# First queries projected ahead of the later values, second modulation vector staged in the context's place

## Chip, cores and metric

The kernel runs on one core of one Trainium2 chip. The metric is the device time of one execution in microseconds (us). The core has a matrix engine (PE, with weight loads shown apart as PEld), a vector engine (DVE), a scalar engine (ACT), GpSimd (POOL), and SyncE (SP), whose queue issues the loads here. Each engine takes its own instructions in the order in which the built program holds them, and an instruction that waits holds up what stands behind it on the same engine.

## The reference

Two trunk layers over 512 latent tokens of width 1024, with a prefix of 256 context tokens. What touches the change is the entry of layer 0:

```python
sh1, sc1, g1, sh2, sc2, g2 = adaln_params(c, mod_w[i], mod_b[i])      # silu(c) @ w + bias, 6 vectors of 1024
h  = modulate(rms_norm(x, norm_g[i, 0]), sh1, sc1)                    # latent tokens
hc = modulate(rms_norm(ctx, norm_g[i, 0]), csh1, csc1)                # context tokens
proj = h @ w_in                                                       # queries of 8 heads, keys and values of 4
q_a = apply_rope(rms_norm(q_a, q_g), cos, sin)                        # heads 0-3, global; keys of this group likewise
k_a = apply_rope(rms_norm(k_a, k_g), cos, sin)
q_b, k_b = apply_rope(q_b), apply_rope(k_b)                           # heads 4-7, windowed, no norm
o_a = attend(q_a, [k_ctx, k_a], [v_ctx, v_a]);  o_b = window_attention(q_b, ...)
y = concat([o_a, o_b]) @ w_out
x = x + g1 * rms_norm(y, norm_g[i, 1])                                # then a gated ConvFFN with sh2, sc2, g2
```

Layer 1 replaces attention by a Fourier mixing. All matrix products are done in three passes on a high and a low part (`mm3`: high by high, high by low, low by high), so every weight and activation is first split: ACT casts the high part (`wh`), DVE or POOL subtracts for the low part (`wl`).

## The kernel before

The input projection of layer 0 runs in two parts. The first (the loop over `START`) makes the modulated latent tokens `hh`/`hl` and context tokens `ch`/`cl` and, as they come, the keys and values of the global group. Then the loop over `kind` (line 835 and on) does three column groups of 256: `kb` (keys of the windowed heads), `vb` (their values) and `qa` (queries of heads 0 and 1). A group takes blocks of two token tiles: two latent blocks, and for `kb` and `vb` a third one of context. A block is 48 matmuls of 128x256 into one PSUM tile `mm`. The `qa` blocks also carry side work: `keys(0)` at the first of them, which transposes the first key head out of `K` (six PE transposes into two `misc` tiles), and splits it into `kh`/`kl`; `values(0)` at the second.

The keys of the global group are normalised late: `kst` holds sums of squares, `rsqrt(krs, ...)` makes the reciprocal roots in a chain of small DVE instructions, and POOL then scales the twelve 128x128 pieces of `K` by `krs` (line 796). `keys(0)` can transpose a piece only when POOL has scaled it.

Beside that runs `gate = gemv_early(...)`: two adaLN vectors (0, 2) and (0, 3) are made on DVE, eight multiply-adds of 128x1024 each (line 472; `scol` holds the activated c), with one load of 512 KB per multiply-add (line 458). The loads lie in five places in turn: three in `yT` (`yf[:, 0..2]`) and two in the place `cT` that the context tokens have left. The first vector gathers in `yf[:, 3]`, the second in `sqx`. `gemv_end` then sums over partitions on PE (line 433), and transposes back (line 443). The loop over `kind` advances this generator by `pump(gate, n)`.

`yT` is also where the queries go: `Q` is a view of it, and `q_out(0, t0, ps)` writes the rotated first queries there (`roped`, lines 741 to 765; the last step on POOL for the first block, on DVE for the second). `queries_t(0)` transposes them for head 0 (line 943), with the queries of heads 2 and 3 (`gm`) projected between.

Order: `SY` issues loads in program order, each waiting until its place is free. A scheduler places the instructions on each engine by priority of code order and by when their buffers come free; the built order is what counts.

Of the kernel before, what the change touches and what calls it, by code (L numbers as in the profile page):

```python
# [21 lines left out]
KC = D // P  # L22
# [54 lines left out]
def kernel(ctx: ExitStack, tc: tile.TileContext, a):  # L77
# [5 lines left out]
    def mk(pool, shape, dt=F32, tag=None, bufs=1):  # L83
        cnt[0] += 1
        n = nbufs.setdefault((id(pool), tag), (pool, bufs))[1]
        return pool.tile(shape, dt, tag=tag, name=f"{tag}_{cnt[0]}", bufs=n)
# [343 lines left out]
    def gemv_end(l, v, acc, pps):  # L430
        ps = mk(pps, [P, T], F32, "misc", 2)
        for j in range(4):
            PE.matmul(ps[32 * j:32 * j + 32, :256], lhsT=ones32, rhs=acc[:, j * 256:(j + 1) * 256], start=True,
                      stop=True)
        rs = acc
        S.copy(out=rs[:, :256], in_=ps[:, :256])
        yield
        gemv_out(l, v, rs, pps)
# [12 lines left out]
    def gemv_early(jobs, places, accs, pps):  # L451
        ws = {}

        def load(n):
            if n < KC * len(jobs):
                (l, v), k = jobs[n // KC], n % KC
                ws[n] = places[n % len(places)]()
                SY.dma_start(out=ws[n], in_=a["mod_r"][6 * l + v - 2, k // 2][:, k % 2, :])

        for n in range(3):  # L460
            load(n)
        yield
        for n in range(3, len(places)):
            load(n)
        yield
        ends = []
        for n in range(KC * len(jobs)):
            acc, k = accs[n // KC], n % KC
            if k == 0:
                V.tensor_scalar(out=acc, in0=ws[n], scalar1=scol[:, 0, k:k + 1], scalar2=None, op0=ALU.mult)  # L470
            else:
                V.scalar_tensor_tensor(out=acc, in0=ws[n], scalar=scol[:, 0, k:k + 1], in1=acc, op0=ALU.mult,
                                       op1=ALU.add)
            load(n + len(places))
            yield
            if k == KC - 1:
                ends.append(gemv_end(*jobs[n // KC], acc, pps))
            elif k in (1, 3):
                for e in ends:
                    next(e, None)  # L480
        yield
        for _ in range(2):
            next(ends[-1], None)
            yield
# [22 lines left out]
    def pump(it, n=1):  # L507
        for _ in range(n):
            next(it, None)
# [12 lines left out]
    with ExitStack() as es:  # L522
# [16 lines left out]
        def keys(kv, parts):  # L539
            b0 = 0  # L540
            for pt, n in parts:
                for b in range(n):
                    PE.transpose(out=pt[:, b * P:(b + 1) * P], in_=K[:, b0 + b, kv * P:(kv + 1) * P], identity=ident)
                split(kh[:, b0 * P:(b0 + n) * P], kl[:, b0 * P:(b0 + n) * P], pt[:, :n * P])
                b0 += n

        def values(kv):
            vh, vl = wpair([P, 6, P])
            split(vh, vl, Vv[:, :, kv * P:(kv + 1) * P])
            return vh, vl  # L550

        with ExitStack() as e1:
# [150 lines left out]
            for s in START.split():  # L703
                n = [int(c) for c in s[1:]]
# [24 lines left out]
            def context_place(i):  # L729
                if not ce:  # L730
                    ce.append(mk(pj, [P, KC, TC], F32, "cT").rearrange("p a b -> p (a b)").rearrange(
                        "p (n d) -> p n d", d=D))
                return ce[0][:, i, :]

            gate = gemv_early([(0, 2), (0, 3)], [lambda i=i: yf[:, i, :] for i in range(3)] + [
                lambda i=i: context_place(i) for i in range(2)],
                [yf[:, 3, :], sqx[:, 0:4, :].rearrange("p a b -> p (a b)")], pps)
# [33 lines left out]
            def k_out(dst, src, t0, is_ctx):  # L771
                if is_ctx:
                    S.copy(out=dst, in_=src)
                else:
                    roped(dst, src, t0, None)
# [23 lines left out]
            def group_weights(g):  # L799
                r = raw([P, KC, 256], a["w_in"][g])  # L800
                out = []
                for i in range(2):
                    wh, wl = wpair([P, 4, 256])
                    split(wh, wl, r[:, 4 * i:4 * i + 4, :])
                    out.append((wh, wl))
                return out

            def project(ps, ws, sh, sl, t0):
                for i in range(2):
                    tk = slice((t0 + i) * P, (t0 + i + 1) * P)  # L810
                    for k in range(KC):
                        wh, wl = ws[k // 4]
                        mm3(ps[:, i, :], sh[:, k, tk], sl[:, k, tk], wh[:, k % 4, :], wl[:, k % 4, :], k == 0,
                            k == KC - 1)
                        if k % 2:
                            yield


            def q_out(qi, t0, ps):
                dst = Q[:, t0:t0 + 2, qi * 256:(qi + 1) * 256]  # L820
                if qi < 2:

                    roped(dst, ps, t0, 0, qst[:, qi, t0:t0 + 2, :].rearrange("p a b -> p (a b)"),
                          V if qi == 0 and t0 else G)
                else:
                    roped(dst, ps, t0, None)
                if qi < 2 and t0:
                    q, r = (v[:, qi, :, :].rearrange("p t h -> p (t h)") for v in (qst, qrs))
                    V.tensor_scalar(out=q, in0=q, scalar1=1.0 / P, scalar2=EPS, op0=ALU.mult, op1=ALU.add)
                    rsqrt(r, q, qtm)  # L830
                    V.tensor_scalar(out=qsc[:, 2 * qi:2 * qi + 2, :].rearrange("p h t -> p t h"),
                                    in0=qrs[:, qi, :, :], scalar1=SCALE, scalar2=None, op0=ALU.mult)

            blocks = [(hh, hl, 0, 2), (hh, hl, 2, 4), (ch, cl, 0, 0)]
            for g, kind in enumerate(["kb", "vb", "qa"]):
                ws = group_weights(g)
                if g == 2:
                    v_kv = []
                if g == 2:
                    w_q = group_weights(3)  # L840
                for sh, sl, t0, kb in (blocks if kind[0] != "q" else blocks[:2]):
                    ps = mk(pps, [P, 2, 256], F32, "mm", 6)
                    pr = project(ps, ws, sh, sl, t0)
                    for _ in range(2):
                        pump(pr, 4)
                        pump(gate, 2 if kind == "vb" else 1)
                    if kind == "vb":
                        S.copy(out=Vv[:, kb:kb + 2, 256:512], in_=ps)
                    elif kind == "kb":
                        k_out(K[:, kb:kb + 2, 256:512], ps, t0, sh is ch)  # L850
                    else:
                        if t0 == 0:
                            keys(0, [(mk(pps, [P, T], F32, "misc", 2), n) for n in (2, 4)])
                        else:
                            v_kv.append(values(0))
                        q_out(0, t0, ps)
# [12 lines left out]
        with ExitStack() as e2:  # L869
# [80 lines left out]
            for head in range(8):  # L950
# [6 lines left out]
                for j in range(TT):  # L957
# [4 lines left out]
                    if is_a:  # L962
# [4 lines left out]
                        reg, n = ps[:, 128:896], NK  # L967
                    else:
# [12 lines left out]
                        reg, n = ps[:, 256:512 + nl], TC + nl  # L981
# [674 lines left out]
```

## Time and profile before

| What | Value |
|---|---|
| median of 3 runs | 1150.75 us (1148.4 to 1152.72) |
| the profiled execution | 1151.45 us, of which span 1149.7 us |
| mean granted TensorE clock | 0.992 |
| DVE, ACT, POOL busy | 877.7, 578.3, 174.0 us (76%, 50%, 15% of the span) |
| loads and stores | 149.51 MB, 130 GB/s over the span |

The span runs from the first to the last instruction of the profiled execution; 1.75 us of that execution's time lie around it. A busy share is an average over stages; what an edit is worth is read in its own stage, here 85 to 150 us of the span.

### The profile page before, as it was taken

What the parts mean: (1) busy time and instruction counts of PE and PEld (TensorE: products, weight loads), DVE (VectorE), ACT (ScalarE), POOL (GpSimd) and SP (SyncE); (2) the same over time, 40 slices, a digit from 0 to 9 for tenths busy, and PEclk for the clock granted to TensorE, in tenths of its full rate; (3) what the DMA queues carried; (4) which work ended last, traced back from release to release, by engine and by line L of the source; (5) the groups of instructions that cost most, each with busy time, mean ns of one, the idle gap of its engine ahead of it and who ended that gap; (6) DMA issues with size and microseconds to landing.
All of it is one profiled execution on the core that took longest, in us unless ns stands there. A gap on an engine that the chain in (4) does not pass through costs nothing.

```text
span 1149.7 us, 19092 instructions
## 1 busy us (share of the span) xinstructions
PE 1117.8 (97%) x7642; PEld 963.9 (84%) x7642; DVE 877.7 (76%) x1422; ACT 578.3 (50%) x1030; POOL 174.0 (15%) x178
## 2 busy tenths in 40 slices
PE   8999999999999999999999998989999999999995
PEld 4689988868888978887998898869887888899895
DVE  4678777765679976987998568988997498679745
ACT  4342356666665633552465445557743355256442
POOL 1236332521420000000000153500000000000023
PEclk9999999999999999999999999999999999999998
DMA  9576101075142355545525300630228123223212
GB/s 366 239 242 214 44 1 38 7 265 205 38 184 111 125 196 198 214 131 201 193 98 191 113 9 15 206 106 35 74 84 281 46 103 111 93 91 111 92 56 74
DMA packets 30881, 149.51 MB, mean 130 GB/s; under 512 B 3140, under 2 KB 7876, under 8 KB 18632
## 3 DMA queue, kind: packets, MB, share of 16 engines
q1 hardware_dynamic: 30792, 148.29, 36.5%
q8 instruction: 60, 0.98, 0.3%
q14 instruction: 29, 0.24, 0.1%
HBM read 144.08 MB, written 4.19 MB: 129 GB/s over the span
## 4 chain that ended last, share of the span: by engine, by line
PE 84%; DVE 8%; ACT 5%; issue 2%; POOL 1%; DMA 0%; DVEq 0%; SPq 0%; ACTq 0%; POOLq 0%
PE mm L99 24%; PE mm L100 23%; PE mm L101 23%; PE PT L914 1%; ACT wh L122 1%; PE mm L174 1%; PE O L99 1%; DVE md_t L291 1%; PE gm L492 1%; PE gm L99 1%; PE O L100 1%; PE gm L101 1%; PE gm L100 1%; PE O L101 1%; PE misc L180 1%
## 5 line engine op out<-in xcount | busy, mean ns | idle before, releaser
L122 ACT CAST wh<-raw 128x1024 fp32r<-128x1024 f32 (+2 forms) x189 | 180.5, 966 | 188.4 <-PE mm L100 128.1
L122 DVE TENSOR_TENSOR wl<-raw,wh 128x1024 fp32r<-128x1024 f32 (+3 forms) x179 | 204.2, 1148 | 63.2 <-ACT wh L122 63.1
L99 PE MATMUL mm<-hh,wh 128*128 128x256 f32 (+2 forms) x652 | 220.8, 339 | 1.4 <-ACT yT L889 0.9
L100 PE MATMUL mm<-hl,wh 128*128 128x256 f32 (+2 forms) x652 | 218.5, 335 | 0.0
L101 PE MATMUL mm<-hh,wl 128*128 128x256 f32 (+2 forms) x652 | 218.4, 335 | 0.0
L266 POOL TENSOR_TENSOR gacc<-gacc,sq 128x256 f32<-128x256 f32 (+1 forms) x35 | 29.9, 855 | 716.0 <-ACT sq L264 715.1
L99 PEld LDWEIGHTS mm<-hh,wh 128*128 128x128 f32 x652 | 122.6, 188 | 18.7 <-ACT sq L1140 2.7
L100 PEld LDWEIGHTS mm<-hl,wh 128*128 128x128 f32 x652 | 122.7, 188 | 14.1
L101 PEld LDWEIGHTS mm<-hh,wl 128*128 128x128 f32 x652 | 122.7, 188 | 14.0
L99 PE MATMUL mm<-xh,wh 128*128 128x512 f32 (+1 forms) x368 | 132.1, 359 | 0.0
L100 PE MATMUL mm<-xl,wh 128*128 128x512 f32 (+1 forms) x368 | 130.9, 356 | 0.0
L101 PE MATMUL mm<-xh,wl 128*128 128x512 f32 (+1 forms) x368 | 130.4, 355 | 0.0
L99 PE MATMUL mm<-zh,wh 128*128 128x256 f32 x304 | 87.0, 286 | 0.0
L100 PE MATMUL mm<-zl,wh 128*128 128x256 f32 x304 | 84.7, 279 | 0.0
L101 PE MATMUL mm<-zh,wl 128*128 128x256 f32 x304 | 84.5, 278 | 0.0
L99 PEld LDWEIGHTS mm<-xh,wh 128*128 128x128 f32 x368 | 69.2, 188 | 12.8 <-issue 2.1
L100 PEld LDWEIGHTS mm<-xl,wh 128*128 128x128 f32 x368 | 69.2, 188 | 11.2 <-issue 0.4
L101 PEld LDWEIGHTS mm<-xh,wl 128*128 128x128 f32 x368 | 69.2, 188 | 10.9
L1200 ACT ACTIVATE cv<-mm,cols 128x512 f32<-128x512 f32 x64 | 49.7, 777 | 26.2 <-PE mm L101 23.3
L99 PEld LDWEIGHTS mm<-zh,wh 128*128 128x128 f32 x304 | 57.2, 188 | 3.5 <-ACT sq L1143 2.7
L101 PEld LDWEIGHTS mm<-zh,wl 128*128 128x128 f32 x304 | 57.3, 188 | 0.0
L1201 DVE SCALAR_TENSOR_TENSOR cv<-mm,cols,cv 128x511 f32<-128x511 f32 x64 | 47.6, 745 | 12.6 <-ACT cv L1200 11.7
(417 smaller groups left out, 2684.8 us busy)
## 6 DMA issues: line engine op xcount, KB each, us to landing
raw<-in_w_up SPq DMA_DIRECT2D x44, 1024.0 KB, 4.9
xT<-in_mod_r SPq DMA_DIRECT2D x20, 1024.0 KB, 5.0
raw<-in_w_down SPq DMA_DIRECT2D x32, 512.0 KB, 3.7
raw<-in_mod_p SPq DMA_DIRECT2D x8, 1024.0 KB, 4.8
raw<-in_w_in SPq DMA_DIRECT2D x6, 1024.0 KB, 7.6
raw<-in_w_down SPq DMA_DIRECT2D x16, 384.0 KB, 3.1
yT<-in_mod_r SPq DMA_DIRECT2D x10, 512.0 KB, 5.9
raw<-in_w_out SPq DMA_DIRECT2D x4, 1024.0 KB, 5.0
```

The lines of the kernel that those rows point to most:

```text
L99: i = PE.matmul(out, lhsT=ah, rhs=bh, start=start, stop=False, skip_group_check=skip)
L100: PE.matmul(out, lhsT=ah, rhs=bl, start=False, stop=False, skip_group_check=skip)
L101: return i, PE.matmul(out, lhsT=al, rhs=bh, start=False, stop=stop, skip_group_check=skip)
L122: i = S.copy(out=h, in_=src), eng.tensor_tensor(out=l, in0=src, in1=f(h), op=ALU.subtract)
L174: PE.matmul(ps[:32, :src.shape[1]], lhsT=ones32, rhs=src, start=True, stop=True)
L180: PE.matmul(ps[32 * j:32 * j + 32, :w], lhsT=ones32, rhs=sq[:, j * w:(j + 1) * w], start=first, stop=last)
L266: G.tensor_tensor(out=self.acc[:, sl], in0=self.acc[:, sl], in1=sq[:, sl], op=ALU.add)
L291: m = V.scalar_tensor_tensor(out=t, in0=yT[:, k, hs], scalar=der[:, l, gi, k:k + 1], in1=R, op0=ALU.mult, op1=ALU.mult)
L492: PE.matmul(ps[32 * q:32 * q + 32, :], lhsT=spad[:, k, :], rhs=w[:, q * T:(q + 1) * T], start=k == 0, stop=k == KC - 1)
L914: PE.transpose(out=pt[:, j * P:(j + 1) * P], in_=Ps[j][:, off:off + P], identity=ident)
L1200: S.activation(out=cv, in_=ps, func=AF.Identity, bias=bc, scale=wc[1])
L1201: V.scalar_tensor_tensor(out=cv[:, 1:], in0=ps[:, :T - 1], scalar=wc[0], in1=cv[:, 1:], op0=ALU.mult, op1=ALU.add)
```

## The change

Two edits. The first is the order of the three column groups: `kb`, then `qa`, then `vb` instead of `kb`, `vb`, `qa`. The weights of each group keep their index; `w_q`, the weights of the next queries, are now asked for in the `vb` round; the double pump of `gate` goes from `vb` to `qa`. `keys(0)` and `values(0)` stay tied to the two `qa` blocks. The second edit is where the loads of the second vector lie: the eight loads of the first vector use the five places as before, those of the second alternate between the two places in `cT`. Loads 8 and 9 are still issued after the multiply-adds 3 and 4; from 10 on, a load is issued after the multiply-add two before it, which empties its place.

```diff
-                ws[n] = places[n % len(places)]()
+                ws[n] = places[n % len(places) if n < KC else 3 + n % 2]()
...
-            load(n + len(places))
+            if n + len(places) < KC:
+                load(n + len(places))
+            for m in {3: (8,), 4: (9,)}.get(n, (n + 2,) if n >= KC else ()):
+                load(m)
...
-            for g, kind in enumerate(["kb", "vb", "qa"]):
+            for g, kind in ((0, "kb"), (2, "qa"), (1, "vb")):
                 ws = group_weights(g)
                 if g == 2:
                     v_kv = []
-                if g == 2:
+                if g == 1:
                     w_q = group_weights(3)
...
-                        pump(gate, 2 if kind == "vb" else 1)
+                        pump(gate, 2 if kind == "qa" else 1)
```

Lines after the loop over `kind` move by three (796 becomes 799, 943 becomes 946).

On PE, at the transposes of the first key head (`misc<-con,K`; `con` holds the identity), the built order before has them at the start of the eighth and last block (`mm_1309`, the second of `qa`), behind the three blocks of `vb` and the first of `qa` (`mm_1228`):

```order
L101 MATMUL mm_1228<-wh_1214,hl_70 128x256
L443 MATMUL misc_1283<-con_66,sqx_159 128x128 x2
L543 MATMUL misc_1287<-con_66,K_81 128x128 x2
L99 MATMUL mm_1309<-wh_1210,hh_69 128x256
L543 MATMUL misc_1288<-con_66,K_81 128x128 x4
L100 MATMUL mm_1309<-wl_1211,hh_69 128x256
```

and now between the first block behind `kb` (`mm_1030`, now `qa`; it stands where the first block of `vb` stood) and the second `qa` block (`mm_1106`):

```order
L99 MATMUL mm_1030<-wh_1026,hh_69 128x256
L100 MATMUL mm_1030<-wl_1027,hh_69 128x256
L101 MATMUL mm_1030<-wh_1026,hl_70 128x256
L546 MATMUL misc_1084<-con_66,K_81 128x128 x2
L546 MATMUL misc_1085<-con_66,K_81 128x128 x4
L99 MATMUL mm_1106<-wh_1022,hh_69 128x256
```

The six transposes move ahead by three blocks of 48 matmuls: seven blocks stood in front of them, now four do.

On DVE, from the last steps of the `krs` chain on, before:

```order
L122 TENSOR_TENSOR wl_1211<-raw_1208,wh_1210 128x1024
L158 TENSOR_TENSOR ktm_760<-krs_759 128x12
L472 SCALAR_TENSOR_TENSOR sqx_159<-cT_874,scol_77,sqx_159 128x1024
L159 SCALAR_TENSOR_TENSOR ktm_760<-ktm_760,kst_758 128x12
L122 TENSOR_TENSOR wl_1215<-raw_1208,wh_1214 128x1024
L160 SCALAR_TENSOR_TENSOR krs_759<-ktm_760,krs_759 128x12
L472 SCALAR_TENSOR_TENSOR sqx_159<-yT_68,scol_77,sqx_159 128x1024
L122 TENSOR_TENSOR wl_1221<-raw_1218,wh_1220 128x1024
L472 SCALAR_TENSOR_TENSOR sqx_159<-yT_68,scol_77,sqx_159 128x1024 x2
L472 SCALAR_TENSOR_TENSOR sqx_159<-cT_874,scol_77,sqx_159 128x1024 x2
```

and now (the multiply-adds of the second vector are the L472 rows, the split of the transposed key the `kl` rows):

```order
L122 TENSOR_TENSOR wl_1175<-V_82,wh_1174 128x768
L158 TENSOR_TENSOR ktm_760<-krs_759 128x12
L472 SCALAR_TENSOR_TENSOR sqx_159<-cT_874,scol_77,sqx_159 128x1024
L159 SCALAR_TENSOR_TENSOR ktm_760<-ktm_760,kst_758 128x12
L122 TENSOR_TENSOR wl_1204<-raw_1201,wh_1203 128x1024
L160 SCALAR_TENSOR_TENSOR krs_759<-ktm_760,krs_759 128x12
L472 SCALAR_TENSOR_TENSOR sqx_159<-cT_874,scol_77,sqx_159 128x1024
L122 TENSOR_TENSOR wl_1208<-raw_1201,wh_1207 128x1024
L472 SCALAR_TENSOR_TENSOR sqx_159<-cT_874,scol_77,sqx_159 128x1024
L752 TENSOR_TENSOR sq_1098<-mm_1030,Rs_749 128x512
L122 TENSOR_TENSOR kl_91<-misc_1084,kh_90 128x256
L122 TENSOR_TENSOR kl_91<-misc_1085,kh_90 128x512
```

Up to the last `krs` step the two differ by one split (768 columns of `V` in place of 1024 of a weight); behind it there are now three long instructions, the first rope product `sq`, and then the `kl` rows.

On PE, the transposes of the first queries stood in two pairs with 29 matmuls of `gm` between them; before:

```order
L101 MATMUL mm_1309<-wh_1214,hl_70 128x256
L943 MATMUL PT_1397<-con_66,yT_68 128x128 x2
L99 MATMUL gm_1404<-wh_1220,hh_69 128x256
L100 MATMUL gm_1404<-wl_1221,hh_69 128x256
L943 MATMUL PT_1397<-con_66,yT_68 128x128 x2
L101 MATMUL gm_1404<-wh_1220,hl_70 128x256
```

and now in one piece behind the last block of `vb` (its context block, `mm_1325`):

```order
L101 MATMUL mm_1325<-wh_1207,cl_161 128x256
L443 MATMUL misc_1380<-con_66,sqx_159 128x128 x2
L946 MATMUL PT_1397<-con_66,yT_68 128x128 x4
L99 MATMUL gm_1404<-wh_1213,hh_69 128x256
```

The number of matmuls, transposes, multiply-adds and loads is the same in both programs.

## Prediction

> **What bounds the kernel now.** I read the page's busy shares and its chain of work that ended last, then the busy times of stretches around the changed code, then PE's waits there.
>
> ```profile
> PE 1117.8 (97%) x7642; PEld 963.9 (84%) x7642; DVE 877.7 (76%) x1422; ACT 578.3 (50%) x1030; POOL 174.0 (15%) x178
> PE 84%; DVE 8%; ACT 5%; issue 2%; POOL 1%; DMA 0%; DVEq 0%; SPq 0%; ACTq 0%; POOLq 0%
> ```
>
> PE is busy 1117.8 of 1149.7 us and holds 84% of the chain; DMA holds none. A microsecond in which PE stands still is lost, unless one of its later waits shrinks by as much.
>
> ```profile
> 90.00:100.00 10.00, 10.00 (x91) 9.73 (x89) 10.00 (x19) 3.05 (x4) 3.91 (x2) 1.00 0.67 211
> 110.00:122.30 12.30, 12.29 (x106) 11.57 (x105) 5.68 (x10) 3.46 (x6) 6.46 (x8) 1.00 0.24 85
> 122.30:135.00 12.70, 11.06 (x87) 10.55 (x86) 11.02 (x27) 3.13 (x5) 2.18 (x3) 1.00 0.24 85
> 135.00:150.00 15.00, 13.62 (x97) 12.46 (x96) 12.50 (x29) 7.96 (x14) 7.58 (x8) 1.00 0.00 1
> 150.00:200.00 50.00, 49.56 (x331) 44.34 (x330) 36.36 (x73) 29.56 (x55) 13.52 (x14) 1.00 0.06 22
> PE PT L943 <- DVE yT L765: 1.6, 1, 1.6
> PE S L101 <- DVE ql L122: 1.2, 1, 1.2
> ```
>
> The first numbers of a stretch are its length and PE's busy time. PE is full through the projections to 122.3 us; then it loses 1.64 us and 1.38 us. The waits name the two: the second pair of transposes of the first queries waits for their rotation (L765), and a score matmul waits for the split of the next queries. So all that this change can win is about 3 us, 0.3%. What a measurement of this kernel can tell from no change is about 0.5%, or 5.75 us.
>
> **What is moved: the key transposes.** The queries bring `keys(0)` with them, so PE comes to the transposes of `K` right behind the fourth block. Blocks differ in their weights alone, so the fourth, which was of `vb`, gives the time.
>
> ```profile
> 91.08 0.28 PE L99 MATMUL mm<-wh,hh 128*128 128x256 f32 x1
> 96.66 0.28 PE L101 MATMUL mm<-wh,hl 128*128 128x256 f32 x1
> 99.77 0.16 DVE L160 SCALAR_TENSOR_TENSOR krs<-ktm,krs 128x12 f32<-128x12 f32 x1
> 100.02 13.27 POOL L796 TENSOR_SCALAR K<-K,krs 128x128 f32<-128x128 f32 x12 [4.58 <-DVE krs L160]
> 115.78 0.38 PE L543 MATMUL misc<-con,K 128*128 128x128 f32 x2
> 116.29 0.63 PE L543 MATMUL misc<-con,K 128*128 128x128 f32 x4
> ```
>
> The block starts at 91.08 and issues its 48th matmul at 96.66; PE is free for the transposes at **96.9**. But POOL begins to scale `K` only at 100.02, behind the last `krs` step, and ends the twelfth piece at 113.29. Before, the transposes stood at 115.78, 2.5 us behind that: a wait that was never seen. Now PE meets it in front. The last transpose needs the eleventh scaled piece (pieces alternate between the two heads). PE takes instructions in order, so the second `qa` block and all of `vb` stand behind it.
>
> When is the eleventh piece ready? DVE's order to the last `krs` step is the old one, but for one subtraction of 768 columns in place of 1024.
>
> ```profile
> 98.63 1.21 DVE L122 TENSOR_TENSOR wl<-raw,wh 128x1024 fp32r<-128x1024 f32 x1
> 138.04 0.96 DVE L122 TENSOR_TENSOR wl<-V,wh 128x768 fp32r<-128x768 f32 x1 [0.43 <-ACT wh L122]
> L796 POOL TENSOR_SCALAR K<-K,krs x12: 369/1204/3589, 100.0 to 112.9; 128x128 f32<-128x128 f32 x12
> 100.02 3.59 POOL L796 TENSOR_SCALAR K<-K,krs 128x128 f32<-128x128 f32 x1 [4.58 <-DVE krs L160]
> 102.18 2.59 DVE L472 SCALAR_TENSOR_TENSOR sqx<-yT,scol,sqx 128x1024 f32<-128x1024 f32 x2
> 104.80 2.61 DVE L472 SCALAR_TENSOR_TENSOR sqx<-cT,scol,sqx 128x1024 f32<-128x1024 f32 x2
> 108.60 1.28 DVE L472 SCALAR_TENSOR_TENSOR sqx<-yT,scol,sqx 128x1024 f32<-128x1024 f32 x1 [1.19 <-DMA yT<-in_mod_r]
> 106.31 3.81 POOL L796 TENSOR_SCALAR K<-K,krs 128x128 f32<-128x128 f32 x5
> ```
>
> So POOL starts at 100.02 - (1.21 - 0.96) = 99.8. One piece takes 0.37 us at least, 1.20 in the median and 3.59 at most: five are done between 106.31 and 110.12, around DVE's idle 1.19 us (107.41 to 108.60), while beside DVE's long instructions of 1.2 to 1.3 us POOL gets about one piece per instruction, and the first took three of them. The bounds: eleven pieces alone end at 99.8 + 11 x 0.37 = **103.9**; at the old pace the eleventh ends at 113.29 - 0.25 - 0.37 = **112.7**.
>
> The new DVE order decides between them. Behind `krs` stand a multiply-add, a weight subtraction and a multiply-add (1.28 + 1.21 + 1.28 = 3.8 us), then a product and a `kl` split out of PSUM (0.69 + 0.41, DVE L749 and L122), and then the second `kl` split, which waits for PE's last transpose, hence for POOL itself. From there DVE is idle until POOL is done. The first multiply-add waits, too: its load has the place that the vector's first multiply-add frees, so it is issued where the first row here was (the next two rows are the product and the `kl` split, the last an early `krs` step for the third rival),
>
> ```profile
> 96.16 0.33 SPq L458 DMA_DIRECT2D cT<-in_mod_r  x1
> cT<-in_mod_r SPq DMA_DIRECT2D x1, 512.0 KB, 4.7
> 116.54 0.69 DVE L749 TENSOR_TENSOR sq<-mm,Rs 128x512 f32<-128x512 f32 x1 [0.40 <-ACT sq L746]
> 117.14 0.41 DVE L122 TENSOR_TENSOR kl<-misc,kh 128x256 fp32r<-128x256 f32 x1
> 89.01 0.17 DVE L164 TENSOR_SCALAR krs<-ktm 128x12 int32<-128x12 int32 x1
> ```
>
> and lands at 96.16 + 4.7 = 100.9. Until then POOL does three pieces alone (99.8 + 3 x 0.37 = 100.9). DVE's three long instructions fill 100.9 to 104.7, in which POOL gets one to three; the other five to seven run alone and end at 106.5 to 107.3. I take **107.0**, nearer to the free pace than to the old one because DVE must fall idle here. PE stands still from 96.9 to 107.0: **+10.1 us**, with ends 7.0 and 15.8.
>
> [...]
>
> **What goes with it.** The six transposes with one matmul between them took 115.78 to 116.67; all but the last now run inside the wait, which gives back **-0.7**. The wait for L765 goes, since the queries are rotated three blocks earlier:
>
> ```profile
> 127.79 0.44 PE L943 MATMUL PT<-con,yT 128*128 128x128 f32 x2 [1.64 <-DVE yT L765]
> ```
>
> **-1.6**. What is late next there is the split of these queries, which waits for the transposes; 48 `gm` matmuls (5.7 us) lie between them and the first scores. The other wait (1.2) keeps its place and releaser: 0, with ends -1.2 and +1.
>
> **The clock.** PE idle for long loses its granted clock.
>
> ```profile
> 755.50:759.50 4.00, 3.15 (x45) 2.09 (x46) 2.06 (x8) 1.69 (x6) 0.00 (x0) 0.61 0.79 277
> 692.00:695.00 3.00, 3.00 (x27) 2.83 (x18) 2.43 (x8) 0.79 (x2) 0.86 (x1) 0.51 0.00 0
> 759.50:760.00 0.50, 0.50 (x3) 0.29 (x2) 0.24 (x2) 0.23 (x1) 0.00 (x0) 0.72 0.01 0
> 693.49 0.41 PE L100 MATMUL mm<-wl,hh 128*128 128x256 f32 x1
> 693.71 0.41 PE L101 MATMUL mm<-wh,hl 128*128 128x256 f32 x1
> ```
>
> The third number from the end is the granted clock. Behind gaps at 753 and 691 us it stands near 0.5 for some 3.4 us of renewed work. In it matmuls of this shape follow each other at 0.22 us (693.49, 693.71) in place of 0.12 (5.58 us for 47 steps in the block above). One such stretch costs 3.4 x (1 - 0.12 / 0.22) = 1.5 us. This gap is longer than those, so the clock is down when work resumes, and recovery may need a second stretch: 3.1. I take **+2.2**.
>
> [...]
>
> **What costs nothing.** The loads of the second vector keep number and size. With two places they come in lockstep with DVE, two multiply-adds at a time; the last is issued some 15 us after the first, and PE needs the sum only two and a half blocks (14 us) behind the second `qa` block. If a load came that much later, PE would wait for the surplus. `vb` comes later, but its values feed heads 4 to 7, whose turn is past 195 us. DVE's `kl` wait holds up the rope of the first `qa` block and one weight split; PE first needs either more than two blocks later. Weight loads issue as early as before or earlier.
>
> **Sum.** 10.1 - 0.7 - 1.6 + 2.2 = **+10.0 us**. Everything behind hangs on PE, so it is passed on. Against the profiled execution (1149.7 span and 1.75 around it): 1151.45 + 10.0 = 1161.4. That execution is 0.7 above the median of 1150.75, so I forecast **1160.8**.
>
> **Rivals.**
> 1. *POOL has it easy.* DVE waits longer for its loads and POOL runs alone: 103.9, a wait of 7.0 us; with a clock loss of 1.5, +6.2, or 1157. For it speaks the 0.37 us; against, three long instructions that have to go through first. Chance 0.17.
> 2. *POOL at the old pace.* 112.7, a wait of 15.8, clock 3.1: +16.6, or 1167. For it speaks the median of 1.20; against, that DVE blocks at `kl`. Chance 0.12.
> 3. *Not slower: the keys are ready in time.* If the `krs` chain ended by 96.9 - 11 x 0.37 = 92.8, 7 us earlier than now, no wait would be left, and the 1.6 us come as a gain: 1149.1. `krs` is started at 89.0, and only DVE's interleaved multiply-adds and splits stretch it over 11 us. But these stand in the new order as well. Chance 0.03.
> 4. *The change does not do what it says for time: the wait is taken back.* It would need some 5 us of later waits that a late PE removes; from 150 to 200 us PE idles 0.44 in all. That leaves +3 to +5, 1155. Chance 0.05.
>
> The forecast case, +8 to +13, has 0.63. The range takes rivals 1 and most of 2: **1156 to 1166**. Faster by over 0.5% 0.01; within 0.5% 0.09 (rivals 3 and 4, and the low edge of 1); slower by over 0.5% 0.90.
>
> **What would show it.** PE's waits list a wait of 7 to 16 us for POOL L799 at the transposes L546, from about 97 us; POOL's pieces run at 0.37 us once DVE waits at `kl`; the granted clock near 0.5 for 3 to 7 us behind it; no wait of L946 for yT; all stages from the first scores on late by about 10 us. If PE runs on at 97 us, or the stages behind come less than 5 us late, I am wrong.

## The result

| What | Before | Changed |
|---|---|---|
| median | 1151.74 us (1148.4 to 1153.32, 4 runs) | 1159.45 us (1158.38 to 1159.63, 4 runs) |
| the profiled execution, its span | 1151.45, 1149.7 us | 1158.38, 1156.6 us |
| TensorE clock of that execution | 0.992 | 0.990 |

The ratio is 1.0073, with a 95% interval of 1.0056 to 1.0090: slower by 0.73%, or 6 to 10 us, where 1160.8 us and a range of 1156 to 1166 were forecast. Between the two medians lie 7.7 us.

The page of the changed kernel, the busy line and the chain that ended last:

```profile
PE 1118.9 (97%) x7642; PEld 965.2 (83%) x7642; DVE 878.1 (76%) x1422; ACT 578.2 (50%) x1030; POOL 169.0 (15%) x178
PE 82%; DVE 8%; ACT 5%; POOL 2%; issue 2%; DMA 0%; DVEq 0%; SPq 0%; ACTq 0%; POOLq 0%
```

The same matmuls take 1118.9 us of PE (1117.8 before); PE's share of the chain fell from 84% to 82% and POOL's rose from 1% to 2%. PE waits, as its list of waits has it (what waits, for whom; total, times, longest):

```profile
PE misc L546 <- POOL K L799: 7.6, 6, 3.3
PE S L101 <- DVE ql L122: 1.2, 1, 1.2
```

The wait of the query transposes (PT) for yT is gone, the one for `ql` is still there, and the new one is at the key transposes. PE's timeline in that place (start, length, line, operation, and in brackets the idle time before it):

```profile
94.32 0.28 PE L101 MATMUL mm<-wh,hl 128*128 128x256 f32 x1
97.93 0.33 PE L546 MATMUL misc<-con,K 128*128 128x128 f32 x1 [3.33 <-POOL K L799]
100.64 0.48 PE L546 MATMUL misc<-con,K 128*128 128x128 f32 x1 [2.38 <-POOL K L799]
...
104.39 0.47 PE L546 MATMUL misc<-con,K 128*128 128x128 f32 x1 [0.22 <-POOL K L799]
104.52 0.56 PE L99 MATMUL mm<-wh,hh 128*128 128x256 f32 x1
```

The fourth block issues its last matmul at 94.32, and the fifth begins at 104.52. Between them PE does six transposes, which the fifth block does not read but stands behind in PE's order; the 7.6 us in the list are the gaps between them, and the rest of the stretch is the transposes themselves. What set that pace, from DVE's timeline, and from POOL the group of twelve pieces (shortest, median and longest piece in ns; start of the first and of the last in us) and the last six on its timeline:

```profile
97.25 0.15 DVE L160 SCALAR_TENSOR_TENSOR krs<-ktm,krs 128x12 f32<-128x12 f32 x1
97.63 1.31 DVE L472 SCALAR_TENSOR_TENSOR sqx<-cT,scol,sqx 128x1024 f32<-128x1024 f32 x1 [0.23 <-DMA cT<-in_mod_r]
98.86 1.21 DVE L122 TENSOR_TENSOR wl<-raw,wh 128x1024 fp32r<-128x1024 f32 x1
101.08 1.28 DVE L472 SCALAR_TENSOR_TENSOR sqx<-cT,scol,sqx 128x1024 f32<-128x1024 f32 x1 [1.00 <-DMA cT<-in_mod_r]
102.28 0.68 DVE L752 TENSOR_TENSOR sq<-mm,Rs 128x512 f32<-128x512 f32 x1
102.88 0.41 DVE L122 TENSOR_TENSOR kl<-misc,kh 128x256 fp32r<-128x256 f32 x1
105.53 0.69 DVE L122 TENSOR_TENSOR kl<-misc,kh 128x512 fp32r<-128x512 f32 x1 [2.23 <-ACT kh L122]
```

```profile
L799 POOL TENSOR_SCALAR K<-K,krs x12: 365/368/2387, 97.5 to 104.3; 128x128 f32<-128x128 f32 x12
102.58 2.10 POOL L799 TENSOR_SCALAR K<-K,krs 128x128 f32<-128x128 f32 x6
```

`krs` is ready at 97.4; then POOL has three long DVE instructions beside it, and only two pieces are long, one beside the first two (2.39 us) and one beside the third (1.35 us, 101.26 to 102.61). The others take 0.37 us: in DVE's pauses, 1.00 us for a load and 2.23 us blocked at `kl`, and also from 102.58 on beside `sq` and the first `kl`, which read one of their inputs from PSUM. The median piece took 0.37 us, against 1.20 before.

### A stage to measure with

The two profiled executions differ by 2.35 us before the changed code begins: ACT copies the third `kb` block at 91.28 before and at 88.93 now. Stages are therefore compared, from that copy (K<-mm) to ACT's square of the first `gm` block (sq<-gm), which has the same PE work between its ends. ACT's timeline of the kernel before:

```profile
91.28 0.59 ACT L773 COPY K<-mm 128x512 f32<-128x512 f32 x1 [0.35 <-PE mm L101]
...
130.68 0.60 ACT L746 ACTIVATE sq<-gm 128x512 f32<-128x512 f32 x1 [1.83 <-PE gm L101]
```

and of the changed kernel:

```profile
88.93 0.59 ACT L776 COPY K<-mm 128x512 f32<-128x512 f32 x1 [0.35 <-PE mm L101]
...
137.41 0.60 ACT L749 ACTIVATE sq<-gm 128x512 f32<-128x512 f32 x1 [4.41 <-PE gm L101]
```

The stage takes 39.40 us before and 48.48 now: **+9.1 us**. Behind it both need 1019 us (1149.7 - 130.68 = 1019.0 and 1156.6 - 137.41 = 1019.2). That the two agree this closely is in part luck, since the other traces, whose code is the same there, need 1017 to 1022; but nothing near 9 us is given back later.

### The profile page after: what moved, and what is told of

It is laid out like the page before. It is cut to its first block, busy times and chain, and to the rows that moved or that the text cites. A ratio compares the mean times of both kernels' runs of the same rounds, so it can differ in the third digit from the quotient of the medians.

```text
span 1156.6 us, 19095 instructions
## 1 busy us (share of the span) xinstructions
PE 1118.9 (97%) x7642; PEld 965.2 (83%) x7642; DVE 878.1 (76%) x1422; ACT 578.2 (50%) x1030; POOL 169.0 (15%) x178
## 4 chain that ended last, share of the span: by engine, by line
PE 82%; DVE 8%; ACT 5%; POOL 2%; issue 2%; DMA 0%; DVEq 0%; SPq 0%; ACTq 0%; POOLq 0%
PE mm L99 23%; PE mm L100 22%; PE mm L101 22%; PE PT L917 1%; ACT wh L122 1%; PE mm L174 1%; PE gm L99 1%; PE gm L101 1%; PE gm L100 1%; PE O L99 1%; DVE md_t L291 1%; PE gm L495 1%; PE O L100 1%; PE O L101 1%; DVE wl L122 1%
```

## The experiments

The time is the median, beside runs of the kernel before on the same chip; the stage is that of the profiled execution, 39.4 before and 48.5 in the changed kernel.

| Run | Stage, us | Time, before beside it, us | Ratio, 95% interval |
|---|---|---|---|
| e2_places | 46.2 | 1158.89, 1150.82 | 1.0069 (1.0050 to 1.0087) |
| e3_keys_late | 43.8 | 1154.18, 1150.82 | 1.0032 (1.0018 to 1.0045) |
| e4_head_first | 45.4 | 1158.29, 1150.82 | 1.0063 (1.0045 to 1.0081) |
| e7_fill | 54.8 | 1164.63, 1150.82 | 1.0120 (1.0099 to 1.0140) |
| e11_fill20 | 47.6 | 1156.97, 1150.93 | 1.0058 (1.0039 to 1.0077) |
| e5_scale_act | 45.4 | 1154.87, 1150.93 | 1.0039 (1.0022 to 1.0056) |
| e10_keys_last | 43.6 | 1152.97, 1150.93 | 1.0026 (1.0014 to 1.0037) |
| e8_both | 38.7 | 1150.40, 1150.93 | 0.9999 (0.9985 to 1.0013) |
| e9_four | 49.4 | 1160.06, 1151.24 | 1.0077 (1.0062 to 1.0091) |
| e12_mm | 37.3 | 1146.66, 1151.24 | 0.9960 (0.9944 to 0.9975) |
| e13_both_again | 39.1 | 1149.61, 1150.99 | 0.9994 (0.9980 to 1.0008) |
| e14_mm_again | 37.3 | 1147.15, 1150.99 | 0.9963 (0.9951 to 0.9975) |

### The places alone

The kernel before with the second edit only: the order of the groups stays kb, vb, qa.

> Only the second edit: the second vector's loads lie in the context's two places, the three column groups keep their old order (kb, vb, qa). Theory (the loss is PE's wait at the key transposes, which the order alone brings): no such wait, all stages as before, 1151.7 us, between 1149 and 1154. Rival (two places in lockstep with DVE make the vector late, and PE pays for that): the sum of the second vector comes late to PE, 1155 or more.

The theory lost. The edit that was to be free costs 6.8 us of the stage when it stands alone. PE's timeline, DVE's list of waits, and the stretches (length, PE's busy time, ...; the third number from the end is the granted clock):

```profile
114.41 1.08 PE L433 MATMUL misc<-sqx,ones 128*32 128x256 f32 x8 [4.51 <-DVE sqx L472]
```

```profile
DVE sqx L472 <- DMA cT<-in_mod_r: 7.8, 4, 4.3
```

```profile
114.41:119.27 4.86, 4.86 (x26) 4.05 (x27) 1.86 (x2) 0.37 (x1) 0.00 (x0) 0.50 0.54 185
```

PE stands 4.5 us at L433, the sum of the second vector over the partitions, because DVE's last multiply-add is late; then 4.9 us go at half clock. A matmul step takes 0.213 us there in place of 0.119, so that costs some 2.1 us, and the two together make 6.6 of the 6.8. DVE itself waits 7.8 us for loads (1.2 before): with two places a load can go out only when the multiply-add two before it is done. In the changed kernel none of this is to be seen. There PE comes to L433 only at 127.31, and the last multiply-add ends at 120.88:

```profile
119.60 1.28 DVE L472 SCALAR_TENSOR_TENSOR sqx<-cT,scol,sqx 128x1024 f32<-128x1024 f32 x1
127.31 0.64 PE L433 MATMUL misc<-sqx,ones 128*32 128x256 f32 x8
```

### The keys moved out of the first query block

```diff
-                        if t0 == 0:
-                            keys(0, [(mk(pps, [P, T], F32, "misc", 2), n) for n in (2, 4)])
-                        else:
+                        if t0:
                             v_kv.append(values(0))
                         q_out(0, t0, ps)
+                    if kind == "vb" and t0 == 2:
+                        keys(0, [(mk(pps, [P, T], F32, "misc", 2), n) for n in (2, 4)])
```

> The changed kernel with the transposes of the first key head taken out of the first query block and put behind the second block of the vb group, where three blocks of PE work cover POOL; everything else as in the changed kernel. Theory: the wait for POOL at L546 (7.6 us by the list of waits, some 10 us of PE standing still) and the half clock behind it go, and the removed wait for yT stays removed: 1151.7 - 1.6 = 1150.1 us, between 1147 and 1153. Rival (the loss is in the order of the groups itself, in the queries' place in yT or the late values): 1156 to 1160.

Between the two: the wait for POOL is gone and the stage falls by 4.6 us, but the time stays 3.4 us above before, where 1.6 below was expected. In its place PE's timeline and DVE's have

```profile
121.20 1.02 PE L433 MATMUL misc<-sqx,ones 128*32 128x256 f32 x8 [4.97 <-DVE kl L122]
```

```profile
117.85 1.28 DVE L472 SCALAR_TENSOR_TENSOR sqx<-cT,scol,sqx 128x1024 f32<-128x1024 f32 x1
...
120.73 1.01 DVE L122 TENSOR_TENSOR kl<-misc,kh 128x256 fp32r<-128x256 f32 x2
```

The vector's sum needs a `misc` tile, and both are held by the transposed keys until DVE has split them (`kl`), which stands behind the late multiply-adds and the root chain of the queries. PE came to L433 at 116.2; the last multiply-add ended only at 119.1. Two causes lie on one wait; the run with the keys last, below, keeps only one of them.

### What in the wait is the late `krs`, and what POOL's pace

Two runs leave the keys in place. In the first POOL scales the six pieces of the first key head before those of the second (the loops over `h` and `b` change places); in the second ACT scales all twelve:

```diff
-                    G.tensor_scalar(out=sl_, in0=sl_, scalar1=krs[:, 2 * b + h:2 * b + h + 1], scalar2=0.0,
-                                    op0=ALU.mult, op1=ALU.add)
+                    S.activation(out=sl_, in_=sl_, func=AF.Copy, scale=krs[:, 2 * b + h:2 * b + h + 1])
```

> The changed kernel with POOL's twelve pieces in another order: the six of the first key head first, then the six of the second. The last transpose then needs the sixth piece in place of the eleventh. From the trace of the changed kernel the sixth piece ends at about 102.7 us, the eleventh at 104.4. Theory (the end of the wait is set by POOL's piece number): the wait ends 1.7 us earlier, 1157.7 us. Rival (the wait hangs on when krs is ready and on DVE's loads, POOL's pieces are cheap): under 0.5 us, 1159.4.

> The changed kernel with the twelve pieces of K scaled on ACT in place of POOL. krs is ready as before, at about 97.3 us, and ACT should need some 0.27 us a piece (0.59 for 128x512, 0.37 for 128x256), so the eleventh at about 100.4 in place of 104.4. Theory (of the ten us, three are the late krs and seven POOL's pace beside DVE): the wait shrinks by 4 us, stage 44.5, 1155.5. Rival (the late krs and the key splits set it, the scaling engine does not matter): stage 48, 1159.4.

Both bring the stage from 48.5 to 45.4, but not in the same way. Counted from the K copy, the fifth block begins 2.3 us earlier with the head's order (1.7 expected; POOL's longest piece was 1.42 us there, not 2.39) and 3.7 us earlier with ACT. The rest is the half clock that PE meets behind the wait, 3.9 us of it in the changed kernel:

```profile
102.25:104.53 2.28, 2.28 (x12) 2.28 (x12) 2.28 (x4) 0.59 (x1) 2.28 (x5) 0.50 0.43 144
100.60:106.18 5.58, 5.53 (x29) 5.33 (x30) 5.58 (x7) 1.42 (x4) 2.03 (x2) 0.50 0.75 267
```

With the head's order (first row) it lasts 2.3 us, with ACT (second row) 5.6 us, which gives one some 0.7 us and takes as much from the other. The time of the head's order, 1158.29, does not show its 3.1 us, and its interval is too wide to say that it differs from the changed kernel's. ACT's group and PE's first transposes:

```profile
L799 ACT ACTIVATE K<-K,krs x12: 384/385/401, 97.2 to 100.4; 128x128 f32<-128x128 f32 x12
```

```profile
97.64 0.33 PE L546 MATMUL misc<-con,K 128*128 128x128 f32 x1 [3.11 <-ACT K L799]
98.23 0.33 PE L546 MATMUL misc<-con,K 128*128 128x128 f32 x1 [0.26 <-ACT K L799]
```

A piece takes 0.385 us from the first to the last (384 to 401 ns, where POOL's took 365 to 2387), and the eleventh starts at about 100.1. The first transpose still waits 3.1 us. So of the ten microseconds 3.1 to 3.3 are the late `krs` chain, which neither scaling engine changes. Some 3 are POOL's waits beside DVE: its two long pieces, 2.39 and 1.35 us, hold 3.0 us more than two of 0.37. The rest, about 3.8, is eleven pieces of scaling.

### The half clock behind the gap

PE gets idle matmuls (32x256, results thrown away) ahead of the key transposes, first 40, then 20. `kl_done` holds DVE's order as in the changed kernel; in the traces one product of the query rotation has another place.

```diff
                         if t0 == 0:
-                            keys(0, [(mk(pps, [P, T], F32, "misc", 2), n) for n in (2, 4)])
+                            busy(mk(pps, [P, T], F32, "mm", 6), f(hh[:, 0, halves[1]]), 20)
+                            kl_done.append(keys(0, [(mk(pps, [P, T], F32, "misc", 2), n) for n in (2, 4)]))
```

> The changed kernel with 40 idle matmuls of 32x256 put on PE ahead of the key transposes (about 0.235 us each, 9.4 us), so that PE is at work where it stood still; results are thrown away; DVE's order is held as it was. Theory (the half clock behind the gap costs some 1.7 us beside the wait): the granted clock stays near 1.0 from 95 to 110 us, the transposes end at the same time, and the blocks behind come 1.5 to 1.9 us earlier: 1157.7 us. Rival (PE would have waited for something else behind the gap anyway, so the clock costs nothing): 1159.4.

> As the run with 40 idle matmuls, but with 20. There they took 17.45 us in place of 9.4 (a 32x256 one of this type is two passes), and so held PE 8 us longer than the keys did. 20 take 8.7 us, which ends before the keys are ready, at about the time of the eleventh piece less 1 us. Theory (half clock behind the gap costs 1.7 us beside the wait): granted clock at 1.0 behind the wait, the wait's end as in the changed kernel, stage 48.5 - 1.7 = 46.8, 1157.7. Rival (behind the gap PE would wait for something else anyway): stage 48.5, 1159.4.

The first run was mis-sized: 40 took 17.45 us, the keys were long ready, and its time tells only that. In the second, PE's timeline (20 matmuls of this type are 40 rows) and the stretch behind the wait:

```profile
94.50 8.82 PE L175 MATMUL mm<-hh,ones 128*32 128x256 f32 x40
...
105.31 0.33 PE L557 MATMUL misc<-con,K 128*128 128x128 f32 x1 [0.37 <-POOL K L811]
```

```profile
105.40:109.40 4.00, 4.00 (x36) 3.45 (x37) 2.48 (x3) 0.86 (x2) 1.88 (x3) 1.00 0.62 252
```

and the same four microseconds in the changed kernel:

```profile
104.50:108.50 4.00, 4.00 (x20) 4.00 (x21) 2.97 (x4) 0.59 (x1) 1.73 (x3) 0.51 0.77 315
```

36 matmuls in place of 20, at clock 1.00 in place of 0.51. The last transpose came 0.92 us later here (105.31 against 104.39), yet the stage is 0.84 us shorter: the half clock costs **1.8 us**.

### One late thing at a time

In the first run the keys stand behind the third `vb` block, after the vector's sum, so that the split cannot hold its tile. The second does this too and gives the second vector four places, the context's two and two new ones, each reloaded after the multiply-add that empties it; the first loads of the new places, 10 and 11, go out after the multiply-adds 5 and 6. The third has four places and leaves the keys where the change puts them.

```diff
+NP = 4
+EARLY = {3: (8,), 4: (9,), 5: (10,), 6: (11,)}
...
-                ws[n] = places[n % len(places) if n < KC else 3 + n % 2]()
+                ws[n] = places[n % 5 if n < KC else 3 + n % NP]()
...
-            for m in {3: (8,), 4: (9,)}.get(n, (n + 2,) if n >= KC else ()):
+            for m in EARLY.get(n, (n + NP,) if n >= KC else ()):
...
+                lambda i=i: context_place(i) for i in range(2)] + [
+                lambda i=i: fresh_place(i) for i in range(NP - 2)],
...
+                    if kind == "vb" and sh is ch:
+                        keys(0, [(mk(pps, [P, T], F32, "misc", 2), n) for n in (2, 4)])
```

> As the run before, but with the changed kernel's two places. Only the vector is late here, and the key split can no longer hold the PSUM tile that the vector's sum needs. Theory (two places make the vector late): PE waits at L433 for the last multiply-add, some 3 us from the traces at hand (end of the last multiply-add 30.0 us behind the K copy, PE there at 27.2), with half clock behind it: stage 41 to 43 us, time 1152 to 1154. Rival (the 5.0 us with the keys behind the second vb block were the key split's alone): no wait at L433, stage 37.8, 1149.2.

> The changed kernel with both suspected costs taken out: the transposes of the first key head stand behind the third vb block, and the second vector's loads take turns in four places (the two of the context and two new ones of 128x1024) in place of two. As stage I take the time from ACT's copy of the third kb block (K<-mm) to ACT's square of the first gm block (sq<-gm): 39.4 us before, 48.5 in the changed kernel, 46.2 with the places alone, 43.8 with the keys behind the second vb block. Theory (there are two late things, the scaled keys and the second vector, and either alone makes PE wait): both waits go, stage 39.4 - 1.6 = 37.8 us, time 1.6 us under before, 1149.2. Rival (the order of the groups costs something of its own): stage over 41, time over 1152.

> The changed kernel with four places for the second vector, the keys where the change has them. Theory (the two late things overlap: while PE waits for the keys the vector catches up, so its two places cost nothing here, though they cost 6.8 us alone): no gain; without pauses for loads DVE runs a multiply-add more beside POOL, so the eleventh piece comes at about 105 us in place of 104.4: stage 48.5 to 49.5, 1159 to 1161. Rival (the two costs add up): stage 42 to 45, 1153 to 1156.

With the late vector alone PE stands 3.2 us at L433. The list puts this wait down to a small instruction of the root chain; the last multiply-add, which ends right beside it at 118.55, is what the sum reads. Behind the wait the clock stays down longer than behind the ten-microsecond gap, 6.1 us, until 124.78:

```profile
117.27 1.28 DVE L472 SCALAR_TENSOR_TENSOR sqx<-cT,scol,sqx 128x1024 f32<-128x1024 f32 x1
118.70 1.08 PE L433 MATMUL misc<-sqx,ones 128*32 128x256 f32 x8 [3.16 <-DVE qtm L159]
```

```profile
118.70:124.78 6.08, 6.08 (x31) 5.27 (x32) 2.29 (x9) 1.42 (x2) 0.00 (x0) 0.50 0.23 97
```

With both late things taken out, the wait at L433 is gone, the stage is 38.7 us and the time that of before: the order of the groups costs nothing of its own. Of the 1.6 us that it should win, 1.3 go to a new wait, of the key transposes for a `misc` tile:

```profile
PE misc L548 <- DVE mods L447: 1.3, 1, 1.3
```

With four places and the keys in front, nothing is won: the stage is 49.4 and PE waits 8.6 us in all for POOL. The two costs do not add up; the wait for the keys covers the late vector.

### A version that beats both

The run with both taken out, with the two `misc` tiles of the keys replaced by `mm` tiles, of which there are six (`"misc", 2` becomes `"mm", 6` in its call of `keys`).

> The run with both costs taken out (keys behind the third vb block, four places), with one more wait taken away: there the transposes of the keys waited 1.26 us for a misc tile that DVE freed late; here they go to two mm tiles, of which six lie in turn. Theory (what is left of the change is the rotation's earlier end): stage 38.7 - 1.3 = 37.5 us, time 1.6 to 2 us under before, 1149, which would be the only version faster than before, though by less than can be told surely. Rival (mm tiles bring a wait of their own, or the removed wait is taken by the next one): stage 38.7, 1150.5.

> The kernel with both costs taken out once more (keys behind the third vb block in misc tiles, four places), beside the next run on the same chip. By the traces its stage is 38.7 us against 39.4 before: 0.7 us under before, 1150.4. Rival: none of its own, it is the yardstick of the next one.

> The version with mm tiles once more. It measured 4.6 us under before (interval 2.9 to 6.4), while its stage in the trace is 37.3 us against 39.4 before, which explains 2.1. Theory (the stage is all, and the rest was the spread between executions): 1.5 to 3 us under before, 1148 to 1149.5, and 1.5 us under the run beside it. Rival (something behind the stage gains another 2.5 us): 4 us or more under before, 1147 or less.

It measured faster than before in both sets, by 0.40% and 0.37%, with intervals that leave out 1, and in the second set its median is 2.5 us under that of its neighbour. ACT's timeline of the second run gives the stage:

```profile
89.17 0.59 ACT L785 COPY K<-mm 128x512 f32<-128x512 f32 x1 [0.35 <-PE mm L103]
...
126.45 0.60 ACT L758 ACTIVATE sq<-gm 128x512 f32<-128x512 f32 x1 [4.36 <-PE gm L103]
```

37.28 us, 2.1 under before. Measured are 4.6 and 3.8 us, so the stage accounts for about half. The rest goes with the granted clock. Over the 71 runs of the kernel before beside these experiments the time follows the mean granted clock of the execution: on average 1147.6 us at 0.995, 1149.3 at 0.994, 1151.7 at 0.991 and 1152.5 at 0.990. The five runs of the second set had 0.994 or 0.995, and lie 1.9 us under the runs of before with the same clock; the six of the first set lie 2.4 us under theirs on average. So some 2 us, 0.2%, belong to the version by its stage. Whether it also brings the higher clock, or eleven runs had it by chance, is not shown.

## Why the prediction was right, and where it was not

- **The wait at the key transposes**, +10.1 from block end to eleventh piece: measured 9.95 us, from 94.44 (one step of 0.12 behind the last matmul) to the last transpose at 104.39. The main parts were right. `krs` came 3 us behind the block, POOL started 3.1 us behind it (2.9 forecast), and the eleventh piece was done some 6.9 us later (7.2 forecast); two pieces were slowed by DVE's three long instructions (one to three forecast) and the last five ran at 0.37 us (five to seven forecast). One part was not where the forecast had it: the first multiply-add waited only 0.23 us for its load, so that POOL began one piece ahead of it and not three, and the pause of 1.00 us came at the second multiply-add. That the pauses add up to about the same is luck.
- **-0.7 and -1.6**: the transposes lie in the wait, and the wait for yT does not return in any run with the new order.
- **The clock**, +2.2: the term that was mis-sized. One half-clock stretch came, not one and a half: 18 matmul steps of 0.213 us in place of 0.119, or 1.7 us, and 1.8 by the run with 20 fillers. A second stretch was not needed, yet one stretch has no fixed size either: behind the waits of these runs PE met 2.3 us of half clock (e4_head_first), 3.9 (here), 4.9 (e2_places), 5.6 (e5_scale_act) and 6.1 (e10_keys_last, behind a shorter gap than here). Counted with the wait, the granted clock is 0.50 for 10.24 us here (98.16 to 108.40) and for 6.8 us in e10_keys_last (118.0 to 124.78), so what PE pays also hangs on how much of such a stretch the wait has used up (6.3 us here, 0.7 there). The length of a gap alone does not tell it: in the kernel before, the clock stands at 0.50 behind a wait of 1.03 us (to 691.67) and at 1.00 behind one of 1.64 us (to 127.79).
- **The sum**: 9.95 - 0.7 - 1.6 + 1.7 = 9.35 against 9.1 in the stage, +10.0 forecast. The medians differ by 7.7 us; the interval, 6 to 10 us, holds the stage's 9.1 and just the forecast.
- **"What costs nothing"**: here the step on the second vector's loads failed. It held that the lockstep of two places is covered by two and a half blocks of PE work. In the changed kernel the loads do cost nothing, but only because PE loses ten microseconds first; with the wait for the keys gone, PE waits 3.2 us at L433 for this vector, and in the old order 4.5. The surplus that the step named as a condition was there all along, and that it did not spoil the forecast is luck. Whoever had repaired the keys alone, by the prediction's sum, would have got back 4.6 to 4.9 us of the stage (e3_keys_late, e10_keys_last), not 10.
- **POOL beside DVE**: the trace shows which instructions stand beside POOL's slow pieces. Beside the two multiply-adds and the subtraction, with both inputs in SBUF, its pieces took 2.39 and 1.35 us; beside `sq` and `kl`, with one input in PSUM, 0.37. The piece of 2.39 us runs on across two of those (97.63 to 100.07), as the one of 3.59 us did across three in the kernel before. POOL's spans are rough, as the legend of the profile says.

The rivals fell by their places: POOL alone (a wait of 7.0) and the old pace (15.8) by the measured 9.95; ready keys by the wait itself; the wait taken back later by the 1019 us that both need behind the stage.

## What to carry to other kernels

Of two edits made together, time each alone: a wait that one brings can cover what the other costs. Repairing the covered one then seems not to pay (here the places alone, 49.4 against 48.5 us of the stage), and repairing the other gives back less than its wait. When work is moved ahead of its producer, count from the producer's end (here `krs`, then eleven pieces on POOL, two of them with 2.39 and 1.35 us beside DVE in place of 0.37) to the consumer's new place, and look in the same way at every buffer whose number shrinks. A split that stands late in one engine's order also holds the PSUM tile that it reads, and so stops PE at an unrelated sum (in e3_keys_late at L433 until 121.20, 2.1 us after the last multiply-add had ended).

## What the runs showed of the hardware

The first 20 us differ between executions of the same code. PE's timeline of nine matmuls there, and the stretch around them with the granted clock, in the kernel before and in the changed one:

```profile
8.79 3.79 PE L174 MATMUL mm<-sqx,ones 128*32 128x256 f32 x9
5.00:14.00 9.00, 7.28 (x97) 3.75 (x95) 2.97 (x11) 3.39 (x8) 0.00 (x0) 0.81 1.00 384
```

```profile
8.16 2.10 PE L174 MATMUL mm<-sqx,ones 128*32 128x256 f32 x9
5.00:14.00 9.00, 7.71 (x106) 4.19 (x105) 4.50 (x14) 4.82 (x11) 1.60 (x2) 1.00 1.00 380
```

The same nine take 3.79 and 2.10 us. In ten of the fourteen profiled executions the K copy comes between 88.9 and 89.2 us, in four (before, e7_fill, e8_both, e12_mm) between 90.5 and 91.3. The kernel before has a granted clock of 0.81 from 5 to 14 us, which is one stretch of 3.4 us at half clock (8.85 to 12.27), and the changed kernel 1.00; over the first 20 us it is 0.91 in the kernel before, and 1.00 in e13_both_again and e14_mm_again, whose K copies come at 88.94 and 89.17. A difference of one or two microseconds between two single executions of this kernel says nothing, and that is why the stage was used. The stretches at 0.50 in the kernel before and in the changed one last 3.41 us each (from 8.85, 691.52 and 756.37 us, and from 698.91 and 763.76), but for the 10.24 us at the key transposes and the one that the end of the program cuts off. How much half clock comes differs between executions also where the code is the same: from 690 to 800 us the mean clock is 0.97 in the kernel before and 0.94 in e8_both. A scaling of 128x128 took 384 to 401 ns on ACT (e5_scale_act), where POOL's took 365 to 2387.
